# Two-layer decoder trunk: smaller first weight pieces with nine warming products, and an output by block transposes with a feature-major last slice

## Chip, cores and metric

One Trainium2 chip, one core of it. The metric is the device time of one execution in microseconds; of several runs the median counts.

## The reference

The kernel computes a decoder trunk of two layers on 256 tokens of width 2048, in float32. Layer 0 is a gated spatial unit, layer 1 a causal attention of 16 heads (with 256 tokens there is one key block, so the selection of blocks selects nothing). Both end alike, and the change is at the first product of layer 0 and in the end of layer 1:

```
h = x @ w_in                                  # layer 0: parts u, v, z
y = (branch of the layer) * silu(z)
x = layer_norm(ALPHA * x + y @ w_out, g, b)
x = x + sigmoid(x @ w_ple_gate) * (p @ w_ple_proj)
```

## The kernel before, in words

**Products.** Each float32 operand is split into a high part rounded to the float32r type and the low rest. A product is three matrix products into the same PSUM bank: high x high, low x high, high x low (the low x low one is left out). ACT makes the high part with a copy (L121, L75, L314), VectorE the low part by a subtraction (L122, L76, L315).

**Weights.** All weights stream in as 1 MB units in one fixed order (`chunks`, L91 to L106). `load_weights` (L110) brings one unit in pieces, SP issuing the DMAs (L120): four pieces of 512 columns for the first three units, two of 1024 for all others. The raw pieces share four buffers (`wr`, L119), the split forms three (`wh`, `wl`). `weights` (L125) keeps two units ahead of the one in use. The framework orders each engine's instructions by program order and readiness, and puts in the waits.

**Order of work.** `row_unit` (L182) is one weight unit of a product whose result has tokens on the partitions: 24 products of 512 columns. `row_slice` (L222) is four units for one slice of 512 output features (two banks, one for each half of the tokens). `column_unit` (L229) and `feature_product` (L239) are the form whose result has features on the partitions: the weights are the stationary operand, and 512 columns carry the high and the low part of the 256 tokens at once; with `joined` they go one after the other into the same 256 columns. `at(n, f)` runs `f` after n more units (`tick`, L158), which is how transposes, loads and stores are put between products.

**The start.** The identity is made on POOL (L133), then PE runs `WARM` = 7 products on it (L297). `load_x` (L303) loads the first two feature tiles of x one at a time, with the first weight unit between them; the first stage (v of layer 0, L335) runs over the 16 tiles k of the contraction with all eight banks open.

**The end.** In `after` (L450) each layer multiplies by `w_out`, normalises, makes the embedding product (`embed`, L477) and the gate product on the normalised and transposed x (`turn`, L254), then sigmoid, product and sum for each slice (L517 to L529). In layer 0 the result is turned by VectorE in 32x32 blocks and written to DRAM and back by POOL's DMAs (`turn_far`, L265). In layer 1 `store` (L540) turns it back with four PE transposes for 256 features, copies them with ACT and sends two output DMAs from SP (L552); for slices 0 to 2 it runs one and two units later, for the last slice at once. The output is laid out features x tokens.

Of the kernel before, what the change touches and what calls it, by code (L numbers as in the profile page):

```python
# [26 lines left out]
AHEAD = 2  # L27
PARTS = 2
POOL_LO = (0, 1)
WARM = 7  # L30
NT4 = 20
NR4 = 12
NT2 = 5
# [7 lines left out]
def decoder_trunk(ctx: ExitStack, tc: tile.TileContext, xT, pT, wv_a, wu_a, wz_a, w_sT, b_s,  # L41
# [13 lines left out]
    def t2(name):  # L55
        return act.tile([P, 512], F32, name=name, tag="t2", bufs=NT2)
# [8 lines left out]
    def bank(name):  # L65
        return psum.tile([P, 512], F32, name=name, tag="bank", bufs=8)
# [21 lines left out]
    def flat(src):  # L88
        return [("", {}, src.rearrange("p (b e) -> p b e", b=4))]

    chunks = []  # L91
    for k in range(KT):
        chunks += flat(wv_a[k])
# [16 lines left out]
    def load_weights():  # L110
        pat, kw, src = chunks[len(ready)]
        hi = wpool.tile([P, D], F32R, name="wh", tag="wh")
        lo = wpool.tile([P, D], F32R, name="wl", tag="wl")
        parts = 4 if len(ready) < 3 else PARTS
        n = D // parts
        for i in range(parts):
            c = slice(i * n, (i + 1) * n)
            b = slice(i * 4 // parts, (i + 1) * 4 // parts)
            raw = wpool.tile([P, D // PARTS], F32, name="wr", tag="wr", bufs=4)[:, 0:n]  # L119
            nc.sync.dma_start(raw.rearrange("p (b e) -> p b e", b=4 // parts), src[:, b])  # L120
            nc.scalar.activation(hi[:, c], raw, AF.Copy)  # L121
            nc.vector.tensor_sub(lo[:, c], raw, f32(hi[:, c]))  # L122
        ready.append((pat, kw, hi, lo))
# [6 lines left out]
        return w  # L130


    ident = consts.tile([P, P], F32, name="ident")  # L133
    make_identity(nc, ident)
    half = consts.tile([P, NM], F32, name="half")
# [18 lines left out]
    def at(units, f, *args):  # L154

        later.append([units, f, args])
# [25 lines left out]
    def row_unit(banks, ks, xs, order=None):  # L182


        NN = len(banks[0])
        pat, kw, wh, wl = weights()
        if pat:
            wh, wl = ([w.rearrange(pat, **kw)[:, i] for i in range(len(ks))] for w in (wh, wl))
            wh, wl = [[w] for w in wh], [[w] for w in wl]
        else:  # L190
            wh, wl = ([[w.rearrange("p (k n c) -> p k n c", k=len(ks), n=NN)[:, i, n] for n in range(NN)]
                       for i in range(len(ks))] for w in (wh, wl))

        def three(i, m, ns):
            k = ks[i]
            c = slice(m * P, (m + 1) * P)
            xh, xl = xs[k][:, 0, c], xs[k][:, 1, c]
            first, last = k == 0, k == KT - 1

            def o(n):  # L200
                return banks[m][n].rearrange("p (b c) -> p b c", b=4) if pat else banks[m][n]

            for n in ns:
                nc.tensor.matmul(o(n), xh, wh[i][n], start=first, stop=False)  # L204
            for n in ns:
                nc.tensor.matmul(o(n), xl, wh[i][n], start=False, stop=False)  # L206
            for n in ns:
                nc.tensor.matmul(o(n), xh, wl[i][n], start=False, stop=last)  # L208

        if order:  # L210
            for m, n in order:
                for i in range(len(ks)):
                    three(i, m, [n])
        else:
            for i in range(len(ks)):
                for m in range(NM):
                    three(i, m, range(NN))
        tick()
# [3 lines left out]
    def row_slice(xs, name="y"):  # L222

        banks = [[bank(name)] for _ in range(NM)]
        for c in range(4):
            row_unit(banks, range(4 * c, 4 * c + 4), xs, both if c == 3 else None)
        return [b[0] for b in banks]
# [23 lines left out]
        nc.scalar.activation(o, ps[:, 0:S], AF.Copy)  # L251
        nc.vector.tensor_add(o, o, ps[:, S:2 * S])

    def turn(xs, j, rows, n="t"):  # L254

        tp = bank("tp")
        for u in range(2):
            f = 2 * j + u
            for m in range(NM):
                nc.tensor.transpose(tp[:, u * S + m * P:u * S + (m + 1) * P],  # L260
                                    rows[f // 4][:, m, (f % 4) * P:(f % 4 + 1) * P], ident)
        t = split(tp, n)
        xs[2 * j:2 * j + 2] = [t[:, u] for u in range(2)]

    def turn_far(xs, n, rows, name):  # L265

# [29 lines left out]

    warm = bank("warm")  # L297
    for _ in range(WARM):
        nc.tensor.matmul(warm[:, 0:P], ident, ident, start=True, stop=True)

    xs = [None] * KT

    def load_x(k):  # L303
        raw = t2("xr")
        if k:
            nc.sync.dma_start(in2(raw), xT[:, k:k + 2, :])
            t = split(raw, "x")
            xs[k:k + 2] = [t[:, u] for u in range(2)]
            return
        t = t4("x").rearrange("p (k h s) -> p k h s", k=2, h=2)  # L310
        for i in range(2):
            c = raw[:, i * S:(i + 1) * S]
            nc.sync.dma_start(c, xT[:, i, :])
            nc.scalar.activation(t[:, i, 0, :], c, AF.Copy)  # L314
            nc.vector.tensor_sub(t[:, i, 1, :], c, f32(t[:, i, 0, :]))  # L315
            xs[i] = t[:, i]
            if i == 0:
                load_weights()
# [16 lines left out]
    for k in range(KT):  # L335
        order = None
        if k < 2:
            order = [(m, n) for n in range(NS) for m in range(NM)]
        elif k == KT - 1:
            order = [(m, n) for m in range(NM) for n in range(NS)]  # L340
        row_unit(vb, (k,), xs, order)
        if k % 2 == 0 and k + 2 < KT:
            load_x(k + 2)
# [106 lines left out]
    def after(i, br):  # L450
# [26 lines left out]
        def embed(n, m):  # L477
            if m == 0:
                pp.append(r4("pp"))
                if n % 2 == 0:  # L480
                    wp[:] = [t.rearrange("p (k n c) -> p k n c", k=2, n=2) for t in weights(1 + n // 2)[2:]]
            ps = bank("pp")
            c = slice(m * P, (m + 1) * P)
            for k in range(2):
                xh, xl = pk[:, k, 0, c], pk[:, k, 1, c]
                nc.tensor.matmul(ps, xh, wp[0][:, k, n % 2, :], start=k == 0, stop=False)
                nc.tensor.matmul(ps, xl, wp[0][:, k, n % 2, :], start=False, stop=False)
                nc.tensor.matmul(ps, xh, wp[1][:, k, n % 2, :], start=False, stop=k == 1)
            nc.scalar.activation(pp[n][:, m, :], ps, AF.Copy)
# [3 lines left out]
        def norm_slice(n):  # L493
            for m in range(NM):
                normalise(R[n], gb[n], m, mv[:, m, 0:1], rs[:, m:m + 1])

        units = [(n, m) for n in range(NS) for m in range(NM)]
        for u in units[:5]:
            embed(*u)
        for n in range(2):  # L500
            norm_slice(n)
            turn(xn, 2 * n, R, "xn")
            turn(xn, 2 * n + 1, R, "xn")
            if n == 0:
                for u in units[5:]:
                    embed(*u)

        def rest(n):
            norm_slice(n)
            turn(xn, 2 * n, R, "xn")  # L510
            turn(xn, 2 * n + 1, R, "xn")

        at(1, rest, 2)
        at(2, rest, 3)

        xo = [None] * KT
        for n in range(NS):  # L517
            y = row_slice(xn, "g")
            last = i == DEPTH - 1
            for m in range(NM):  # L520
                parts = 2 if last and n == NS - 1 else 1
                w = 512 // parts
                t = t2("sg")
                for h in range(parts):
                    c = slice(h * w, (h + 1) * w)
                    r = R[n][:, m, c]
                    nc.scalar.activation(t[:, c], y[m][:, c], AF.Sigmoid)
                    nc.vector.tensor_mul(t[:, c], t[:, c], pp[n][:, m, c])
                    nc.vector.tensor_add(r, r, t[:, c])  # L529
            if not last:  # L530
                turn_far(xo, n, R, "xt")
                continue
            for h in range(2):
                if n < NS - 1:
                    at(1 + h, store, 2 * n + h)
                else:
                    store(2 * n + h)
        return xo

    def store(j):  # L540

        tp = bank("to")
        for u in range(2):
            f = 2 * j + u
            for m in range(NM):
                nc.tensor.transpose(tp[:, u * S + m * P:u * S + (m + 1) * P],
                                    R[f // 4][:, m, (f % 4) * P:(f % 4 + 1) * P], ident)
        t = t2("o")
        nc.scalar.activation(t, tp, AF.Copy)
        for u in range(2):  # L550
            f = 2 * j + u
            nc.sync.dma_start(out[f * P:(f + 1) * P, :], t[:, u * S:(u + 1) * S])  # L552

    xs = after(0, br)

# [145 lines left out]
```

## Time and profile before

| what | value |
|---|---|
| median of 3 runs | 1047.32 us (1047.27 to 1048.29) |
| profiled execution, its own time | 1048.48 us |
| its span, first to last instruction | 1046.8 us |
| PE busy | 1035.7 us, 99% |
| VectorE (DVE), ScalarE (ACT), GpSimd (POOL) busy | 650.3, 496.0, 70.2 us |
| DMA, mean over the span | 202 GB/s |

How to read it: times are in us from the start of the span. PE is the matrix product, PEld the load of its stationary operand, which runs beside it; SPq is SP's queue, which issues DMAs. A product's row gives start and duration, and products overlap: the distance between starts is what one costs. What ends an engine's idle time stands in brackets as its releaser. Durations are those of one profiled execution.

### The profile page before, as it was taken

Reading aid. Unit: us, or ns where it says so; the run is one execution under the profiler, and the core shown is the slowest. Engines: PE = TensorE matmul, PEld = TensorE weight load, DVE = VectorE, ACT = ScalarE, POOL = GpSimd, SP = SyncE. Lnnn points to the kernel's source line nnn. Section 1 sums busy time; section 2 is a strip of 40 time slices with the busy share of each in tenths; the row PEclk is TensorE's granted clock in tenths of the full one; section 3 lists DMA queues with packets and bytes.
Section 4 is the critical chain, followed back from the end, with each engine's and each line's share of the span. In section 5 each row is a group of like instructions: output and inputs, shape, how many; then the busy total and the mean of one; then the engine's idle time right before and its main releaser. Section 6 shows DMA issues by size and latency. Waiting matters only on the chain.

```text
span 1046.8 us, 13390 instructions
## 1 busy us (share of the span) xinstructions
PE 1035.7 (99%) x5080; PEld 872.0 (83%) x5080; DVE 650.3 (62%) x849; ACT 496.0 (47%) x679; POOL 70.2 (7%) x116
## 2 busy tenths in 40 slices
PE   8999999999999999999999999999999999999997
PEld 6888888888888878888888888888888888888886
DVE  5666774566465696675546666666666555568552
ACT  5545444444353364543435455555555443345442
POOL 1100100023300002233000000000000000000000
PEclk9999999999999999999999999999999999999999
DMA  7775777678965546779655545545555555554651
GB/s 258 261 250 186 254 216 219 190 214 264 298 218 201 195 166 197 252 235 286 232 189 179 180 162 169 171 163 163 172 175 175 199 195 192 188 199 163 208 195 41
DMA packets 104144, 211.23 MB, mean 202 GB/s; under 512 B 25312, under 2 KB 27632, under 8 KB 104080
## 3 DMA queue, kind: packets, MB, share of 16 engines
q1 hardware_dynamic: 99152, 196.64, 57.2%
q0 software_dynamic: 4928, 13.74, 4.7%
q8 instruction: 40, 0.66, 0.3%
q14 instruction: 24, 0.20, 0.1%
HBM read 204.53 MB, written 5.82 MB: 201 GB/s over the span
## 4 chain that ended last, share of the span: by engine, by line
issue 53%; PE 36%; DMA 7%; DVE 2%; POOL 1%; ACT 1%; POOLq 0%; SPq 0%; ACTq 0%; DVEq 0%
PE g L206 4%; PE g L204 4%; PE g L208 4%; PE u L206 3%; PE u L204 3%; PE u L208 3%; PE z L204 2%; PE v L206 2%; PE z L208 2%; PE v L208 2%; PE z L206 2%; PE v L204 2%; DMA xt<-xtb 2%; DMA wr<-in_wv_a 2%; DMA xtr<-xt 2%
## 5 line engine op out<-in xcount | busy, mean ns | idle before, releaser
L122 DVE TENSOR_TENSOR wl<-wr,wh 128x1024 fp32r<-128x1024 f32 (+1 forms) x366 | 432.9, 1205 | 269.9 <-ACT wh L121 265.1
L121 ACT ACTIVATE wh<-wr 128x1024 fp32r<-128x1024 f32 (+1 forms) x366 | 371.9, 1040 | 381.2 <-PE y L206 130.9
L247 PE MATMUL f<-xt,wh 128*128 128x512 f32 x768 | 271.0, 396 | 0.0
L247 PE MATMUL f<-xt,wl 128*128 128x256 f32 x768 | 206.2, 279 | 0.0
L247 PEld LDWEIGHTS f<-xt,wh 128*128 128x128 f32 x768 | 143.2, 188 | 29.9
L247 PEld LDWEIGHTS f<-xt,wl 128*128 128x128 f32 x768 | 144.5, 188 | 2.9
L204 PE MATMUL g<-wh,xn 128*128 128x512 f32 x256 | 101.1, 395 | 0.0
L208 PE MATMUL g<-wl,xn 128*128 128x512 f32 x256 | 99.9, 390 | 0.0
L206 PE MATMUL g<-wh,xn 128*128 128x512 f32 x256 | 99.7, 390 | 0.0
L204 PE MATMUL y<-wh,b 128*128 128x512 f32 x160 | 62.2, 389 | 0.0
L206 PE MATMUL y<-wh,b 128*128 128x512 f32 x160 | 62.2, 389 | 0.0
L208 PE MATMUL y<-wl,b 128*128 128x512 f32 x160 | 62.2, 389 | 0.0
L208 PEld LDWEIGHTS g<-wl,xn 128*128 128x128 f32 x256 | 48.1, 188 | 10.1
L206 PEld LDWEIGHTS g<-wh,xn 128*128 128x128 f32 x256 | 48.1, 188 | 9.5
L204 PEld LDWEIGHTS g<-wh,xn 128*128 128x128 f32 x256 | 48.1, 188 | 9.5
L204 PE MATMUL u<-wh,x 128*128 128x512 f32 x128 | 49.9, 390 | 0.0
L206 PE MATMUL u<-wh,x 128*128 128x512 f32 x128 | 49.9, 390 | 0.0
L204 PE MATMUL z<-wh,x 128*128 128x512 f32 x128 | 49.8, 389 | 0.0
L206 PE MATMUL z<-wh,x 128*128 128x512 f32 x128 | 49.8, 389 | 0.0
L208 PE MATMUL u<-wl,x 128*128 128x512 f32 x128 | 49.8, 389 | 0.0
L208 PE MATMUL z<-wl,x 128*128 128x512 f32 x128 | 49.8, 389 | 0.0
L204 PE MATMUL v<-wh,x 128*128 128x512 f32 x128 | 38.7, 399 | 2.3 <-ACT wh L121 2.3
(156 smaller groups left out, 1398.0 us busy)
## 6 DMA issues: line engine op xcount, KB each, us to landing
wr<-in_wqkz_b SPq DMA_DIRECT2D x96, 512.0 KB, 3.6
wr<-in_w_out SPq DMA_DIRECT2D x64, 512.0 KB, 4.5
wr<-in_w_gate SPq DMA_DIRECT2D x64, 512.0 KB, 4.4
wr<-in_wu_a SPq DMA_DIRECT2D x32, 512.0 KB, 4.5
wr<-in_wz_a SPq DMA_DIRECT2D x32, 512.0 KB, 5.1
wr<-in_wv_b SPq DMA_DIRECT2D x32, 512.0 KB, 4.8
wr<-in_wv_a SPq DMA_DIRECT2D x26, 512.0 KB, 5.1
gb<-vecs POOLq DMA_DIRECT2D x24, 256.0 KB, 8.0
```

The source lines that it names most:

```text
L121: nc.scalar.activation(hi[:, c], raw, AF.Copy)
L122: nc.vector.tensor_sub(lo[:, c], raw, f32(hi[:, c]))
L204: nc.tensor.matmul(o(n), xh, wh[i][n], start=first, stop=False)
L206: nc.tensor.matmul(o(n), xl, wh[i][n], start=False, stop=False)
L208: nc.tensor.matmul(o(n), xh, wl[i][n], start=False, stop=last)
L247: nc.tensor.matmul(*m, start=k == 0 and j == 0, stop=k == KT - 1 and j == len(ms) - 1, skip_group_check=True)
```

## The change

`WARM` goes from 7 to 9, and the warming products run on a tile of ones that VectorE sets, instead of the identity. The first four weight units are loaded into buffers of the larger pool (`r4`, 12 buffers, one piece each); the first in five pieces (256, 256, 512, 512, 512 columns), the next three in two pieces. The first x tile's DMA goes to ACT's queue. The first slice of the first unit is done in two halves of 256 columns. At the end, slices 0 to 2 are turned by VectorE block transposes and stored by POOL DMAs straight to the output. The last slice is computed feature-major: its embedding, its gate product (two banks with high and low columns side by side, two joined), and a kept transposed copy of the normalised x; it is stored by four DMAs from SP. `store` is gone.

```diff
-WARM = 7
+WARM = 9
+    FIRST = (0, 256, 512, 1024, 1536, D)
...
-        parts = 4 if len(ready) < 3 else PARTS
-        n = D // parts
-        for i in range(parts):
-            c = slice(i * n, (i + 1) * n)
-            b = slice(i * 4 // parts, (i + 1) * 4 // parts)
-            raw = wpool.tile([P, D // PARTS], F32, name="wr", tag="wr", bufs=4)[:, 0:n]
-            nc.sync.dma_start(raw.rearrange("p (b e) -> p b e", b=4 // parts), src[:, b])
+        early = len(ready) < 4
+        bounds = FIRST if not ready else range(0, D + 1, D // PARTS)
+        for c0, c1 in zip(bounds, bounds[1:]):
+            c = slice(c0, c1)
+            raw = r4("wr0").rearrange("p m c -> p (m c)") if early else wpool.tile(
+                [P, D // PARTS], F32, name="wr", tag="wr", bufs=4)
+            raw = raw[:, 0:c1 - c0]
+            if early:
+                nc.sync.dma_start(raw, src.rearrange("p b e -> p (b e)")[:, c])
+            else:
+                nc.sync.dma_start(raw.rearrange("p (b e) -> p b e", e=512), src[:, c0 // 512:c1 // 512])
...
+    ones = consts.tile([P, P], F32, name="ones")
+    nc.vector.memset(ones, 1.0)
...
+            if cols:
+                w = [t[i][ns[0]][:, cols] for t in (wh, wl)]
+                for j, (x, y) in enumerate(((xh, w[0]), (xl, w[0]), (xh, w[1]))):
+                    nc.tensor.matmul(o(ns[0])[:, cols], x, y, start=cols.start == 0 and j == 0, stop=False,
+                                     skip_group_check=True)
+                return
...
-    def turn(xs, j, rows, n="t"):
+    def turn(xs, j, rows, n="t", keep=None):
...
+        if keep is not None:
+            nc.scalar.activation(keep[j // 2][:, j % 2, :], tp, AF.Copy)
...
-        nc.tensor.matmul(warm[:, 0:P], ident, ident, start=True, stop=True)
+        nc.tensor.matmul(warm[:, 0:P], ones, ones, start=True, stop=True)
...
-            nc.sync.dma_start(c, xT[:, i, :])
+            (nc.sync if i else nc.scalar).dma_start(c, xT[:, i, :])
...
+            if k == 0:
+                order[0:NM] = [(m, 0, slice(c, c + S)) for c in (0, S) for m in range(NM)]
...
+        def embed_features(n, m):
...
+            ps = bank("pp")
+            for u in range(2):
+                o = ps[:, u * S:(u + 1) * S]
+                c = slice((2 * m + u) * P, (2 * m + u + 1) * P)
+                for k in range(2):
+                    wh, wl = (w[:, k, n % 2, c] for w in wp)
+                    nc.tensor.matmul(o, wh, pk[:, k, 0, :], start=k == 0, stop=False)
+                    nc.tensor.matmul(o, wh, pk[:, k, 1, :], start=False, stop=False)
+                    nc.tensor.matmul(o, wl, pk[:, k, 0, :], start=False, stop=k == 1)
+            nc.scalar.activation(pp[n][:, m, :], ps, AF.Copy)
...
         for n in range(NS):
+            if last and n == NS - 1:
+                final_slice(n, xn, keep[n], pp[n])
+                return
             y = row_slice(xn, "g")
...
+                if last:
+                    store_blocks(n, m, r)
...
+    def store_blocks(n, m, r):
+        t = t2("ob")
+        nc.vector.transpose(t, r)
+        for g in range(4):
+            c = slice(m * P + 32 * g, m * P + 32 * g + 32)
+            nc.gpsimd.dma_start(out[512 * n:512 * n + 512, c].rearrange("(b c) t -> c b t", c=32),
+                              t[32 * g:32 * g + 32, :].rearrange("p (b t) -> p b t", t=32))
+
+    def final_slice(n, xn, r, pp):
+        banks = [bank("g") for _ in range(4)]
+        joined = [b >= 2 for b in range(4)]
+        for c in range(4):
+            pat, kw, wh, wl = weights()
+            wh, wl = (w.rearrange("p (b k c) -> p b k c", **kw) for w in (wh, wl))
+            ks = range(4)
+            if c < 3:
+                for k in ks:
+                    for b in range(4):
+                        feature_product(banks[b], wh[:, b, k, :], wl[:, b, k, :], xn, 4 * c + k, joined[b])
+                tick()
                 continue
+            for b in range(4):
+                for k in ks:
+                    feature_product(banks[b], wh[:, b, k, :], wl[:, b, k, :], xn, 4 * c + k, joined[b])
+            tick()
+        qs = [t2("sg")[:, 0:S] for _ in range(4)]
+
+        def finish(b):
+            q = qs[b]
+            x = r[:, b // 2, (b % 2) * S:(b % 2 + 1) * S]
+            nc.scalar.activation(q, banks[b][:, 0:S] if joined[b] else q, AF.Sigmoid)
+            nc.vector.tensor_mul(q, q, pp[:, b // 2, (b % 2) * S:(b % 2 + 1) * S])
+            nc.vector.tensor_add(x, x, q)
+            f = 4 * n + b
+            nc.sync.dma_start(out[f * P:(f + 1) * P, :], x)
+
+        for b in range(2):
+            halves_sum(qs[b], banks[b])
+        for b in range(4):
+            finish(b)
```

## Rows read from the trace of the kernel before

**Rows 1.** Waits of the whole run: engine, line, waited for, us in total, times, longest.

```profile
PE v L204 <- ACT wh L121: 2.3, 3, 1.1
PE warm L299 <- POOL ident masks.py:199: 1.6, 1, 1.6
PE to L546 <- DVE r L529: 1.4, 1, 1.4
```

**Rows 2.** Timeline, first 14 us: start, duration, engine, line, operation, idle before and releaser.

```profile
0.80 0.20 POOL masks.py:197 MEMSET ident<- 128x128 f32 x1 [0.29 <-POOLq L693]
0.81 1.28 ACT L314 ACT_TABLE_LOAD   x1 [0.81 <-PEq L693]
0.81 0.38 SPq L313 DMA_DIRECT2D xr<-in_xT  x1
...
1.57 3.35 PE L299 MATMUL warm<-ident 128*128 128x128 f32 x14 [1.57 <-POOL ident masks.py:199]
...
3.12 0.42 ACT L314 ACTIVATE x<-xr 128x256 fp32r<-128x256 f32 x1 [1.02 <-DMA xr<-in_xT]
...
5.03 0.63 ACT L121 ACTIVATE wh<-wr 128x512 fp32r<-128x512 f32 x1 [1.50 <-DMA wr<-in_wv_a]
...
5.71 0.80 PE L204 MATMUL v<-wh,x 128*128 128x512 f32 x1 [0.78 <-ACT wh L121]
...
9.72 0.46 PE L204 MATMUL v<-wh,x 128*128 128x512 f32 x1
```

**Rows 3.** Windows, start: length, busy us (count) of PE, PEld, DVE, ACT, POOL, clock, DMA, GB/s.

```profile
2.00:8.00 6.00, 5.22 (x19) 4.41 (x19) 2.49 (x4) 3.01 (x7) 2.13 (x6) 1.00 0.90 302
8.00:10.00 2.00, 2.00 (x6) 1.58 (x5) 1.94 (x5) 1.58 (x4) 0.00 (x0) 1.00 0.89 276
```

**Rows 4.** Timeline of PE, where the second stage (u) begins.

```profile
97.02 0.39 PE L204 MATMUL u<-wh,x 128*128 128x512 f32 x1
...
100.42 0.39 PE L204 MATMUL u<-wh,x 128*128 128x512 f32 x1
```

**Rows 5.** Timeline of PE, last stage: the last product before each of two stores.

```profile
1022.00 0.39 PE L208 MATMUL g<-wl,xn 128*128 128x512 f32 x1
...
1027.92 0.39 PE L208 MATMUL g<-wl,xn 128*128 128x512 f32 x1
```

**Rows 6.** Timeline of PE in the feature-major stage, and its weight loads (ns min/median/max).

```profile
640.58 0.69 PE L618 MATMUL ov<-pb,vk 128*128 128x256 f32 x5
641.11 0.45 PE L247 MATMUL f<-xt,wh 128*128 128x512 f32 x1
641.40 0.28 PE L247 MATMUL f<-xt,wl 128*128 128x256 f32 x1
...
643.14 0.28 PE L247 MATMUL f<-xt,wl 128*128 128x256 f32 x1
```

```profile
L247 PEld LDWEIGHTS f<-xt,wl x768: 187/188/192, 554.9 to 846.5; 128*128 128x128 f32 x192
```

**Rows 7.** The chain that ended last, its end; then the output DMAs of the tile out.

```profile
1039.72 0.39 ACT sg L527
...
1040.13 0.76 DVE sg L528 x2
```

```profile
L552 SPq DMA_DIRECT2D out<-o x16: 332/410/1460, 978.3 to 1043.8; - x16
...
DMA to landing us min/median/max: 1.7/1.8/3.4
```

**Rows 8.** Tile xtb, the block transposes of layer 0; then a window of the last stage.

```profile
L277 POOL DMA_DIRECT2D xt<-xtb x32: 648/651/709, 403.6 to 475.8; - x32
L273 DVE STREAM_TRANSPOSE xtb<-r x8: 711/711/712, 402.6 to 472.9; 128x512 f32<-128x512 f32 x8
...
DMA to landing us min/median/max: 2.3/4.1/6.1
```

```profile
972.00:994.00 22.00, 22.00 (x102) 18.22 (x101) 12.21 (x12) 9.43 (x12) 0.00 (x0) 1.00 0.63 206
```

More of the change, by code (lines that the diff above doesn't have):

```diff
@@ L192, in row_unit, with three @@
                        for i in range(len(ks))] for w in (wh, wl))
-        def three(i, m, ns):
+        def three(i, m, ns, cols=None):
             k = ks[i]
@@ L201, in o @@
                 return banks[m][n].rearrange("p (b c) -> p b c", b=4) if pat else banks[m][n]
+            if cols:
[4 more added lines that the diff above has]
+                return
             for n in ns:
-                nc.tensor.matmul(o(n), xh, wh[i][n], start=first, stop=False)
+                nc.tensor.matmul(o(n), xh, wh[i][n], start=first, stop=False, skip_group_check=NN == NS)
             for n in ns:
-                nc.tensor.matmul(o(n), xl, wh[i][n], start=False, stop=False)
+                nc.tensor.matmul(o(n), xl, wh[i][n], start=False, stop=False, skip_group_check=NN == NS)
             for n in ns:
-                nc.tensor.matmul(o(n), xh, wl[i][n], start=False, stop=last)
+                nc.tensor.matmul(o(n), xh, wl[i][n], start=False, stop=last, skip_group_check=NN == NS)
         if order:
-            for m, n in order:
+            for m, n, *cols in order:
                 for i in range(len(ks)):
-                    three(i, m, [n])
+                    three(i, m, [n], *cols)
         else:
@@ L495, in norm_slice @@
                 normalise(R[n], gb[n], m, mv[:, m, 0:1], rs[:, m:m + 1])
+        def embed_features(n, m):
+            if m == 0:
+                pp.append(r4("pp"))
+                if n % 2 == 0:
+                    wp[:] = [t.rearrange("p (k n c) -> p k n c", k=2, n=2) for t in weights(1 + n // 2)[2:]]
+            ps = bank("pp")
[8 more added lines that the diff above has]
+            nc.scalar.activation(pp[n][:, m, :], ps, AF.Copy)
@@ L497, in after, with fill, turn_slice @@
+        last = i == DEPTH - 1
+        def fill(n, m):
+            (embed_features if last and n == NS - 1 else embed)(n, m)
         units = [(n, m) for n in range(NS) for m in range(NM)]
         for u in units[:5]:
-            embed(*u)
+            fill(*u)
+        keep = [None] * NS
+        def turn_slice(n):
+            norm_slice(n)
+            end = last and n == NS - 1
+            if end:
+                keep[n] = r4("xf")
+            turn(xn, 2 * n, R, "xn", keep if end else None)
+            turn(xn, 2 * n + 1, R, "xn", keep if end else None)
@@ L500, in after @@
         for n in range(2):
-            norm_slice(n)
-            turn(xn, 2 * n, R, "xn")
-            turn(xn, 2 * n + 1, R, "xn")
+            turn_slice(n)
             if n == 0:
                 for u in units[5:]:
[L506 to L514, printed above, removed]
+                    fill(*u)
+        at(1, turn_slice, 2)
+        at(2, turn_slice, 3)
@@ L516, in after @@
         xo = [None] * KT
         for n in range(NS):
+            if last and n == NS - 1:
+                final_slice(n, xn, keep[n], pp[n])
+                return
             y = row_slice(xn, "g")
-            last = i == DEPTH - 1
             for m in range(NM):
-                parts = 2 if last and n == NS - 1 else 1
-                w = 512 // parts
                 t = t2("sg")
[L524 to L529, printed above, removed]
+                r = R[n][:, m, :]
+                nc.scalar.activation(t, y[m], AF.Sigmoid)
+                nc.vector.tensor_mul(t, t, pp[n][:, m, :])
+                nc.vector.tensor_add(r, r, t)
+                if last:
+                    store_blocks(n, m, r)
@@ L530, in after @@
             if not last:
                 turn_far(xo, n, R, "xt")
-                continue
[L533 to L552, printed above, removed]
+        return xo
```

## The prediction, made before the changed kernel ran

> **What bounds the kernel now.** I read the windows first, then the waits of PE, then the timeline at both ends. In a stretch of the last gate stage PE is busy 22.00 of 22.00 us [rows 8], so in the middle of the kernel only PE's own work counts. The waits of PE [rows 1] lie at its two ends: 1.6 us before the warming products, 2.3 us in the first stage in three pieces, 1.4 us before the last transposes; a fourth, in the layer norms, the change leaves alone.
>
> The start [rows 2]: the warming products wait for the identity that POOL makes and begin at 1.57. They are over at 4.92, and the first real product comes at 5.71, when the first 256 KB weight piece has landed and ACT has rounded it (5.03 plus 0.63). From there nine products of 512 columns start before 9.72, one in about 0.43 us, which is 1.2 GHz; later ones start every 0.2267 us (15 between the two rows of [rows 4]), which is 2.4 GHz. The clock column prints 1.00 all along [rows 3], so the level is read from the spacing.
>
> How late is PE by the end of the first stage? It has 16 weight rows x 24 = 384 products, 87.05 us at 0.2267, and the next stage starts at 97.02 [rows 4]: 9.97 us late. Of that 5.71 is the wait for the first product; nine products in 4.01 us instead of 2.04 are 2.0; the two later waits for ACT (2.3 less the 0.8 before 5.71) are 1.5; the rest, 0.7, goes in restarts.
>
> The end [rows 7]: after the last product the chain is sigmoid 0.39, two VectorE products and the sums, six transposes, two copies, four output DMAs one behind the other. From the sigmoid's start at 1039.72 to the end of the span (1046.8) it is 7.1 us; the last output DMA starts at 1043.8, 3.0 us before the end.
>
> **Part 1, the start.** The ones are set by VectorE, which has nothing before them. POOL's memset of the same size starts at 0.80 and takes 0.20 [rows 2], so PE begins near 1.05. Seven products took 3.35 us, 0.48 each; nine take 4.3 and end near 5.35, but as a product starts about 0.2 before its predecessor's end (0.39 long, 0.2267 apart [rows 4]) the first real one can start at **5.1**.
>
> Are its data there? The x piece (128 KB) was issued at 0.81 and used at 3.12. Now it leaves on ACT's queue while a 128 KB weight piece leaves on SP's at the same moment. The second 131 KB at the 302 GB/s of [rows 3] add 0.43: both by 3.55. ACT rounds them in 0.42 each: 4.4. If ACT's table load of 1.28 stands ahead of its DMA, x lands near 4.4 and the piece is ready at 5.25, 0.15 late. The bounds are 5.1 and 5.7, no gain at all; I take 5.1.
>
> The slow level: no row decides when the clock rises once the break between 4.92 and 5.71 is gone. At one end it rises with the first real product and costs 0. At the other it rises at 9.72 as before: 4.6 us of slow products cost 2.2. I take the middle, 1.1. The six first products split into twelve of half the columns cost 0.1 by [rows 6].
>
> The later waits: the first pieces had to share four raw buffers, so SP held them back; now the eleven pieces of the first four rows have buffers of their own (of the larger pool, idle then), and SP issues them without a wait. The bytes up to the first half of row 1 (1.84 MB) flow at 302 GB/s from 2.0 [rows 3] and land near 8.1; ACT needs twice the 0.63 of a piece half as large [rows 2], VectorE about as long, so both forms are ready near 10.7. Row 1 is wanted near 11.6 (5.1, 24 products of 0.2267 and the 1.1). Row 2 and the x that goes with it come with 1 to 2 us to spare. I put 0.3 for waits; the bounds are 0 and the 1.5 of before. Queued behind these pieces on SP is only what is wanted later.
>
> Late after the change: 5.1 + 1.1 + 0.3 + 0.1 = 6.6 instead of 9.97: **gain 3.4**, between 0.2 (5.7, 2.2, 1.5, the restarts) and 4.9.
>
> **Part 2, stores of slices 0 to 2.** Six times four transposes leave PE. Between the two L208 rows of [rows 5] lie 24 products and one store: 5.92 us, where 24 x 0.2267 is 5.44. A store costs 0.48, its restart included; six are **2.9 gained**. At nothing I cost what takes their place. VectorE gets six block transposes of 0.71 (the same operation in layer 0 [rows 8]); weight differences queue behind them, but VectorE is busy 12.21 of 22 us there, and the weights run two units ahead. POOL gets 24 DMA issues of 0.65, 15.6 us, in a stage where it is idle. SP loses twelve stores, and with them its waits for ACT, ahead of weight loads that nobody was late for. ACT loses eight copies and gets two (the kept transposes). Without that cover a late weight row would stop PE; the same layout in layer 0 shows no wait of PE [rows 1, 8].
>
> Those stores write runs of 128 bytes. The row shows 4.1 us for 64 KB in layer 0 [rows 8] against 1.8 for 128 KB in the old stores [rows 7]. The Trainium skill (DMA: Bandwidth & Descriptors, Specifications) says that transfers below 512 bytes cost a read-modify-write; the trace agrees that they are slow, and by that page alone the last gate stage could lose what part 2 gives. The sum goes by the rows: slice 3 takes some 22 us, the last stores before it 4.1 to 6.1 [rows 8], so none of them ends last.
>
> **Part 3, the last slice, feature-major.** Same columns, more and shorter products. For b below 2 there are 32 pairs of 512 and 256 columns; five pairs take 1.74 us [rows 6], 0.348 against 0.340 for 768 columns in the old form: 32 x 0.008 = 0.26. For the joined ones, 96 products of 256: the attention's five (four of 256, one of 128) take 0.53 from start to start [rows 6], 0.118 per 256 columns, so 32 x (0.354 - 0.340) = 0.45. The embedding of that slice: 24 x 0.118 less 12 x 0.2267 = 0.11. Together **0.8 lost**, between 0 and 1.6.
>
> **Part 4, the tail.** After the last product: sigmoid 0.39, product 0.38, sum 0.38, with handoffs 1.2 us; then one DMA, 3.0 from issue to the end as before. The other three blocks are done during the last products (each bank's last ones take 1.4 us). 4.2 instead of 7.1: **2.9 gained**, between 1.3 (a landing of 3.4 instead of 1.8 [rows 7]) and 3.2.
>
> **Sum.** 3.4 + 2.9 - 0.8 + 2.9 = 8.4 us. The profiled execution took 1048.48 us (span 1046.8): 1040.1. The median of the three runs shown is 1.16 lower, 1047.32; I take that difference as common to both kernels and forecast **1038.9**. If it lies in the slow level of the start, up to 1.2 of the gain is missing.
>
> **Rivals.**
> - *The start gives nothing*: the weight stream, not the held-back issue, sets the first stage's waits, and the clock rises no sooner. For it: 302 and 276 GB/s were moved [rows 3] in the very stretch before PE's waits for weights. Against it: PE needs 1 MB of weights in 5.44 us, 193 GB/s. Gain 8.4 - 3.2 = 5.2: 1042.1. Also the case in which the warming does not do what it is for.
> - *Weight loads show* (slower). The last slice has 160 products instead of 96 and its embedding 24 instead of 12: 76 more weight loads of 0.188 us [rows 6]. If they can't hide behind products of 256 columns they cost 14.3 in the place of the 0.8: -5.1, 1052.4. Over the 152 short products the gain is used up from a spacing of 0.118 + 0.055 = 0.17 us on. Against it: the five attention products each load weights of their own and keep 0.118. The Trainium skill (TensorE: Matmul & The Clock Gate, Part 3, What overlaps and what doesn't) states that a load overlaps running products only where the row group differs, and gives 107 ns a load (LDWEIGHTS); an estimate by that page is 8.1 lost, a gain of 1.1. The trace disagrees: 0.188 of load and 0.213 of columns fit in a spacing of 0.2267.
> - *Block stores hold up weights*: short runs on the same DMA engines give back the 2.9 of part 2: 1041.8. Against it: layer 0, above.
>
> **How the numbers follow.** Forecast 0.82, start gives nothing 0.10, block stores 0.03, weight loads 0.03, several small shortfalls together 0.02. A measurement of this kernel tells 0.2% (2.1 us) from no change. So faster 0.95, same 0.02, slower 0.03. The terms' bounds, not all at one end, make 1036.5 to 1041.5 for the forecast; taken up to the first rival with a little beyond, and off the unlikely low end, the range is 1036.8 to 1042.6.
>
> **What would show it.** Warming from near 1.05; the first real product near 5.1 with no break before it; the first row of the next stage near 93.6 instead of 97.02; no wait for ACT between 10 and 30 us; 24 products per weight unit in 5.44 us in slices 1 and 2; the last slice 0.7 longer; 4.2 us from the last sigmoid to the end. A first stage that still ends near 97, or 256-column products over 0.13 apart, would make the prediction wrong.

## The result, and the profile after

| | before | changed |
|---|---|---|
| median (range, runs) | 1047.3 us (1046.51 to 1048.29, 6) | 1041.32 us (1040.80 to 1041.55, 6) |
| profiled execution, own time | 1048.48 us | 1041.33 us |
| its span | 1046.8 us | 1039.6 us |

The ratio is 0.9944 (0.9934 to 0.9954): 6.0 us faster, inside the range, 2.4 us short of the forecast 1038.9. The profiled execution of before stood 1.16 us above its median; that of the changed kernel stands at its own.

The waits of PE, which answer to [rows 1]:

```profile
PE tp L276 <- DVE r L380: 1.1, 2, 0.6
PE warm L317 <- DVE ones L141: 1.1, 1, 1.1
PE v L223 <- DVE wl L129: 0.5, 1, 0.5
PE v L219 <- ACT wh L128: 0.5, 1, 0.5
```

The wait at the end (1.4 us, for the last sums) is gone, the one ahead of the warming products is 0.5 shorter, and the one in the layer norms (tp) is left. The first stage still waits, now twice and half a microsecond each. Where, the timeline of the first 14 us shows, which answers to [rows 2]:

```profile
0.80 0.40 ACTq L331 DMA_DIRECT2D xr<-in_xT  x1
...
1.12 4.21 PE L317 MATMUL warm<-ones 128*128 128x128 f32 x18 [1.12 <-DVE ones L141]
...
1.23 1.28 ACT L332 ACT_TABLE_LOAD   x1 [1.23 <-PEq L760]
...
3.78 0.42 ACT L332 ACTIVATE x<-xr 128x256 fp32r<-128x256 f32 x1 [1.26 <-DMA xr<-in_xT]
...
4.98 1.16 PE L215 MATMUL v<-wh,x 128*128 128x256 f32 x4
...
5.98 0.40 PE L215 MATMUL v<-wl,x 128*128 128x256 f32 x2
...
6.93 0.40 PE L219 MATMUL v<-wh,x 128*128 128x512 f32 x1
...
8.30 0.63 ACT L128 ACTIVATE wh<-wr 128x512 fp32r<-128x512 f32 x1 [2.13 <-DMA wr<-in_wv_a]
...
8.99 0.50 PE L219 MATMUL v<-wh,x 128*128 128x512 f32 x1 [0.50 <-ACT wh L128]
...
11.11 1.06 ACT L128 ACTIVATE wh<-wr 128x1024 fp32r<-128x1024 f32 x1 [0.93 <-DMA wr<-in_wv_a]
...
13.49 0.50 PE L223 MATMUL v<-wl,x 128*128 128x512 f32 x1 [0.53 <-DVE wl L129]
...
13.82 0.39 PE L219 MATMUL v<-wh,x 128*128 128x512 f32 x1
```

The x piece leaves ahead of ACT's table load, the warming begins at 1.12, and the first real product follows it at 4.98 without a break. From about 5.9 the short products come every 0.12 us: the 2.4 GHz level, long before the 9.72 of [rows 2]. Then PE catches up with its weights. ACT sits idle for 2.13 us until the fourth piece lands and rounds it at 8.30; the first half of the next row, which I had landing near 8.1, is rounded only from 11.11. From 6.93 to 13.82 PE takes 6.89 us for 21 steps that cost 4.76 at 0.2267.

The windows of the same stretch, columns as in [rows 3], and the first product of the next stage (97.02 in [rows 4]):

```profile
2.00:8.00 6.00, 6.00 (x33) 5.82 (x33) 1.79 (x4) 2.18 (x5) 1.91 (x6) 1.00 0.84 239
8.00:10.00 2.00, 1.50 (x6) 0.64 (x5) 0.78 (x2) 1.38 (x3) 0.00 (x0) 1.00 1.00 369
```

```profile
94.77 0.39 PE L219 MATMUL u<-wh,x 128*128 128x512 f32 x1
```

In 2:8 the DMA engines moved 239 GB/s, not the 302 of before, and were busy 0.84 of the stretch. The first stage ends 2.25 us earlier than in the profile of before, where I forecast 3.4.

The end, first the chain that ended last (start, duration), then the output's two kinds of stores with their landing, which answer to [rows 7, 8]:

```profile
1027.94 7.61 PE g L262 x54
1035.55 0.02 issue
1035.57 0.39 ACT sg L610
1035.96 0.02 issue
1035.99 0.43 DVE sg L611
1036.42 0.03 issue
1036.45 0.42 DVE xf L612
```

```profile
L584 POOL DMA_DIRECT2D out<-ob x24: 648/650/705, 970.1 to 1020.2; - x24
L614 SPq DMA_DIRECT2D out<-xf x4: 332/358/431, 1033.5 to 1036.9; - x4
```

```profile
L581 DVE STREAM_TRANSPOSE ob<-r x6: 711/711/714, 969.1 to 1017.3; 128x512 f32<-128x512 f32 x6
...
DMA to landing us min/median/max: 2.3/2.8/4.9
```

From the last sigmoid at 1035.57 to the end of the span it is 4.0 us instead of 7.1. The block stores are over long before it: issued by 1020.9, landing 4.9 us at most.

By the profiles, span against span (7.2 us): the start gave 2.25, the tail 3.05, and the middle, from 94.77 to 1035.57 against 97.02 to 1039.72, 1.90.

### The profile page after: what moved, and what is told of

Read it like the earlier page. It is cut to its first block, busy times and chain, and to the rows that moved or that the text cites. A ratio compares the mean times of both kernels' runs of the same rounds, so it can differ in the third digit from the quotient of the medians.

```text
span 1039.6 us, 13497 instructions
## 1 busy us (share of the span) xinstructions
PE 1032.2 (99%) x5134; PEld 873.0 (84%) x5134; DVE 653.2 (63%) x855; ACT 492.2 (47%) x672; POOL 84.0 (8%) x140
## 4 chain that ended last, share of the span: by engine, by line
issue 44%; PE 9%; DMA 3%; DVE 2%; POOL 1%; ACT 0%; POOLq 0%; DVEq 0%
PE g L262 2%; PE g L223 2%; PE g L221 2%; PE g L219 2%; DMA xtr<-xt 2%; DMA xt<-xtb 1%; DVE wl L129 0%; POOL xt L295 0%; PE tp L276 0%; DVE xt L76 0%; DVE sg L569 0%; DVE r L570 0%; DVE xtb L291 0%; ACT xt L75 0%; POOL rs L491 0%
## 5 line engine op out<-in xcount | busy, mean ns | idle before, releaser
L219 PE MATMUL g<-wh,xn 128*128 128x512 f32 x224 | 87.9, 393 | 0.0
L223 PE MATMUL g<-wl,xn 128*128 128x512 f32 x224 | 87.2, 389 | 0.0
L221 PE MATMUL g<-wh,xn 128*128 128x512 f32 x224 | 87.2, 389 | 0.0
L223 PEld LDWEIGHTS g<-wl,xn 128*128 128x128 f32 x224 | 42.0, 188 | 8.8
L221 PEld LDWEIGHTS g<-wh,xn 128*128 128x128 f32 x224 | 42.1, 188 | 8.5
L219 PEld LDWEIGHTS g<-wh,xn 128*128 128x128 f32 x224 | 42.1, 188 | 8.4
L491 POOL TENSOR_TENSOR rs<-rs,half 128x2 f32<-128x2 f32 x2 | 2.3, 1146 | 541.2 <-DVE rs L490 541.2
```

The costliest lines, as they stand in the source:

```text
L223: nc.tensor.matmul(o(n), xh, wl[i][n], start=False, stop=last, skip_group_check=NN == NS)
L491: nc.gpsimd.tensor_tensor(rs, rs, half, op=ALU.pow)
```

## The experiments

Each kernel was timed beside the kernel before; "changed" is the kernel of the change, 1041.32.

**The two halves apart.** The changed start with the old end, and the old start with the changed end:

```diff
-                if last:
-                    store_blocks(n, m, r)
+            for h in range(2):
+                if n < NS - 1:
+                    at(1 + h, store, 2 * n + h)
+                else:
+                    store(2 * n + h)
...
-    def final_slice(n, xn, r, pp):
...
```

> The changed start with the old end. My theory: the change's gain is three separate pieces, in the two profiles 2.25 us at the start (second stage begins at 94.77 instead of 97.02), 1.9 in the middle and 3.05 in the tail. Then the second stage begins near 94.8 here, and the rest of the run is the old one: 1.1 to 2.3 us faster than before (1045.0 to 1046.2), the lower figure if the profile of before drew a slow start. Rival: the start's gain is lost again behind, because PE only waits elsewhere: the same time as before. Rival 2: the start is worth the 3.4 us forecast: 1043.9.

Measured: 1046.49 us (1045.61 to 1047.37, 11 runs), ratio 0.9991 (0.9982 to 1.0). The start alone gains 0.8 us by the medians, less than I expected and hardly clear of the noise (the interval reaches 1.0), though its profile begins u at 94.76, as the changed kernel's does.

```diff
+                if last:
+                    store_blocks(n, m, r)
...
+    def final_slice(n, xn, r, pp):
...
```

> The old start with the changed end (block stores of slices 0 to 2, feature-major last slice). My theory: 1.9 + 3.05 = 4.95 us faster than before, near 1042.3, with the second stage still beginning near 97. Rival: the two parts need each other, and the end alone gives under 3.5 us (over 1043.8).

Measured: 1042.50 us (1042.42 to 1043.08, 5 runs), ratio 0.9955 (0.9943 to 0.9967): 4.8 us, as expected. The surprise is in its start, whose code is the one of before. Its timeline of PE:

```profile
5.34 0.69 PE L204 MATMUL v<-wh,x 128*128 128x512 f32 x1 [0.41 <-ACT wh L121]
5.87 0.40 PE L206 MATMUL v<-wh,x 128*128 128x512 f32 x1
6.10 0.46 PE L208 MATMUL v<-wl,x 128*128 128x512 f32 x1
6.40 0.40 PE L204 MATMUL v<-wh,x 128*128 128x512 f32 x1
6.63 0.39 PE L206 MATMUL v<-wh,x 128*128 128x512 f32 x1
...
95.45 0.39 PE L204 MATMUL u<-wh,x 128*128 128x512 f32 x1
```

The same start runs at 2.4 GHz from 5.87 on (0.23 us between starts), where the profile of before got there at 9.72, and begins u at 95.45 instead of 97.02. So 1.57 us of the old start differ between two executions of the same code (0.37 of it is the first product, at 5.34 instead of 5.71). Against this draw the changed start (94.77) is worth 0.7.

**Two warming products fewer.**

```diff
-WARM = 9
+WARM = 7
```

> The changed kernel with seven warming products instead of nine; they end 0.9 us earlier, near 4.4, and leave a gap of some 0.5 us before the first real product near 4.9. My theory: the unbroken warming is what lets the products space out at the 2.4 GHz level from 5.98 on; with the gap the 1.2 GHz level lasts longer in some runs, up to near 9.7 as in the kernel before, and costs 0 to 1.9 us, so the median is 0.3 to 1.5 us above the changed kernel and the runs scatter more. Rival: the level rises at the same time, and PE then only waits longer for weights: the same time within 0.3 us.

Measured: 1041.38 us (1041.14 to 1041.81), ratio 0.9944 (0.993 to 0.9957): the same as changed. Seven products end as the data arrive, and the first real one starts at 4.59; the pieces behind it come little sooner (the first half of unit 1 is rounded from 10.80 instead of 11.11).

**Stores by PE again, slices 0 to 2; the last slice stays as changed.**

```diff
-                if last:
-                    store_blocks(n, m, r)
+            if last:
+                for h in range(2):
+                    at(1 + h, store, 2 * n + h)
...
```

> The changed kernel with slices 0 to 2 of the output stored as before, by PE transposes, and the last slice feature-major as in the change. My theory: each of the six stores costs PE 0.48 us, so 2.9 us above the changed kernel (near 1044.2). Rival: the block stores' small runs slow the weights or the tail and give part of it back, so that going back costs under 1.5 us.

Measured: 1044.49 us (1044.29 to 1045.6, 8 runs), ratio 0.9973 (0.9962 to 0.9983). The block stores are worth 3.2 us; the forecast had 2.9.

**The last slice as before, block stores kept.**

```diff
-            (embed_features if last and n == NS - 1 else embed)(n, m)
+            embed(n, m)
...
-                final_slice(n, xn, keep[n], pp[n])
...
+            elif n == NS - 1:
+                for h in range(2):
+                    store(2 * n + h)
```

> The changed kernel with the last slice as before: tokens on the partitions, PE transposes and copies in its tail. Slices 0 to 2 keep the block stores. My theory: the tail is 3.05 us longer, the last slice 1.1 and its embedding 0.1 shorter, so 1.85 us above the changed kernel (near 1043.2). Rival: the longer products of the feature-major form eat what the tail gives: the same within 0.5 us.

Measured: 1043.23 us (1043.02 to 1043.37), ratio 0.9959 (0.9946 to 0.9973): 1.9 slower than changed. Its chain at the end:

```profile
1034.52 0.39 ACT sg L569
...
1034.94 0.76 DVE sg L570 x2
1035.70 0.35 DVE r L571
...
1036.09 0.56 PE to L597 x3
```

From the start of u (94.81) to the last sigmoid it is 939.71 us, in the changed kernel 940.80: feature-major costs 1.1. From there to the end it is 7.0 against 4.0: the tail gives 3.0. The difference, 1.9, is what the medians show.

**What holds the weights of the first stage.** Three kernels tried the causes I thought of first. Units 1 to 3 loaded as before, through the four shared buffers:

```diff
-        early = len(ready) < 4
-        bounds = FIRST if not ready else range(0, D + 1, D // PARTS)
+        early = not ready
+        parts = 4 if len(ready) < 3 else PARTS
+        bounds = FIRST if not ready else range(0, D + 1, D // parts)
```

> The changed kernel, but weight units 1 to 3 loaded as before (four pieces of 512 columns for units 1 and 2, four shared raw buffers), so that SP holds them back. Theory A: the eleven pieces issued at once are what makes the last pieces of unit 0 late (its fourth piece is rounded at 8.30 in the changed kernel, at 7.4 in the kernel before); then the fourth piece is there before 7.6, the wait of PE near 9 goes, and the waits of before near 19 and 26 (together 1.5 us) come back: within 1 us of the changed kernel either way. Rival B: the DMA rate from 3.5 to 7 us (about 200 GB/s) does not depend on what is queued behind; the fourth piece still comes near 8.3, and the time is 1 to 2 us above the changed kernel because both kinds of waits are there.

Measured: 1041.96 us (1041.17 to 1042.61), ratio 0.9948 (0.9935 to 0.996). The fourth piece is rounded at 7.38 instead of 8.30, which fits an early queue that delays it; one execution is little to go by, as the changed start gave 8.12 to 8.82 in three other profiles of this section. PE still waits 0.8 us in two places, and the time is within 1 us of changed. Holding SP back had cost next to nothing.

POOL's two small loads (the column vectors and the spatial bias) moved behind ten units:

```diff
+    at(10, load_small)
```

> The changed kernel with POOL's two small loads (gains and biases, 48 and 8 KB, issued at 1.6 and 2.8 us and under way until about 7.5) put off by ten weight units. Theory A: these loads are what holds the DMA engines near 200 GB/s between 3.5 and 7 us; without them the fourth piece of unit 0 is rounded before 7.2 instead of 8.30, unit 1's first half before 10.2 instead of 11.1, the two waits of PE (0.5 each) and the slips around them go, the second stage begins near 92.9 instead of 94.8, and the time is 1 to 2 us below the changed kernel (1039.3 to 1040.3). Rival B: the slow stretch belongs to the weight DMAs themselves; the pieces land at the same times and the time is the same within 0.3 us.

Measured: 1041.59 us (1041.11 to 1041.98), ratio 0.9943 (0.9931 to 0.9956). It told nothing: the framework orders by readiness, and issued them at 1.98 and 3.20 all the same. So they were tied behind the x of rows 4 and 5, by a write that depends on it:

```diff
+            if k == 4:
+                for o in (colp, bsp):
+                    nc.vector.tensor_scalar(o, raw[:, 0:P], 0.0, None, op0=ALU.mult)
+                nc.gpsimd.dma_start(...)
```

> The changed kernel with POOL's two small loads tied behind the arrival of x for k = 4 (after 12 us), by clearing their tiles with a product of that x and zero; merely moving them in the program had left them at 2.0 and 3.2 us. Theory A: these loads hold the DMA engines near 200 GB/s between 3.5 and 7 us; without them unit 0's fourth piece is rounded before 7.5 instead of 8.30, PE's waits near 9 and 13 go, and the time is 1 to 2 us below the changed kernel. Rival B: the slow stretch belongs to the weight DMAs; the fourth piece stays within 0.5 us of 8.3 and the time within 0.4 us.

Measured: 1041.12 us (1040.71 to 1041.52), ratio 0.9941 (0.9929 to 0.9953). Now the first is issued at 22.0, and the windows are those of the changed kernel:

```profile
2.00:8.00 6.00, 6.00 (x32) 5.87 (x32) 1.79 (x4) 2.18 (x5) 0.24 (x1) 1.00 0.78 243
```

243 GB/s where it was 239, and the fourth piece at 8.34. The small loads are not the cause.

**The shape of the pieces.** The first unit in four pieces of 512 columns, with the products unchanged:

```diff
-    FIRST = (0, 256, 512, 1024, 1536, D)
+    FIRST = (0, 512, 1024, 1536, D)
```

> The changed kernel with the first weight unit in four pieces of 512 columns, without the two of 256. My theory: the first real product waits for 256 KB and comes near 5.4 to 5.7 instead of 4.98, but PE is later held by unit 0's fourth piece and unit 1's first half anyway, so the time is within 0.5 us of the changed kernel. Rival: every tenth lost at the first product is lost at the end: 0.4 to 0.7 us slower.

Measured: 1040.10 us (1039.89 to 1040.38), ratio 0.9929 (0.9917 to 0.9942). It is 1.2 faster than changed (the ranges of the two do not overlap), against what every theory of mine said. Its timeline and windows:

```profile
5.13 1.22 PE L215 MATMUL v<-wh,x 128*128 128x256 f32 x4
...
8.09 0.63 ACT L128 ACTIVATE wh<-wr 128x512 fp32r<-128x512 f32 x1 [1.11 <-DMA wr<-in_wv_a]
...
9.99 1.06 ACT L128 ACTIVATE wh<-wr 128x1024 fp32r<-128x1024 f32 x1 [0.92 <-DMA wr<-in_wv_a]
```

```profile
2.00:8.00 6.00, 6.00 (x30) 5.81 (x30) 2.50 (x4) 2.72 (x5) 1.92 (x6) 1.00 0.94 284
8.00:10.00 2.00, 2.00 (x10) 1.63 (x9) 1.03 (x2) 0.99 (x3) 0.00 (x0) 1.00 1.02 413
```

The first product is 0.15 later, but 284 GB/s flow instead of 239, the next unit's half is rounded at 9.99 instead of 11.11, and no wait of PE in the first stage is left in the list: u begins at 93.66, 1.11 before the changed kernel. A 256-column piece is read in runs of 1 KB a row (256 values of 4 bytes), a 512-column one in runs of 2 KB. To tell the length of the runs from the number of DMAs, one short run kept with four DMAs, and long ones with three:

```diff
+    FIRST = (0, 256, 1024, 1536, D)
```

> The changed kernel with unit 0 in four pieces of 256, 768, 512 and 512 columns: one small piece in front, as many DMAs as the run with four pieces of 512 that took 1040.10. Theory A: what the two small pieces cost is one more DMA in SP's row, 0.46 us later for all that follows; with four DMAs the time is that of the four pieces of 512, 1040.1, or a little below as the first product has its data sooner. Rival B: the 1 KB runs of a small piece are what moves badly; with one of them left the time lies half way, 1040.5 to 1041.

Measured: 1040.72 us (1040.18 to 1041.44), ratio 0.9938 (0.9926 to 0.995). With four DMAs and one 1 KB run it stands half way, 267 GB/s in 2:8 and u at 94.03. That speaks for the runs and against the count alone; but a 768-column piece also changes when each bank's data come, so it is half an answer. Nor can it be the slow transfer of the small pieces alone: most of what is missing is missing from 5 to 8 us (232 GB/s in the changed kernel, 301 with four pieces of 512), when both small pieces are there already (rounded from 4.10).

```diff
+    FIRST = (0, 512, 1024, D)
```

> The changed kernel with unit 0 in three pieces of 512, 512 and 1024 columns. Theory A (number of DMAs in SP's row): everything behind comes another 0.45 us sooner, unit 1's first half is rounded near 9.5 instead of 9.99 with four pieces and 11.11 with five, and the time is 0.2 to 0.5 us below 1040.1. Rival: the last half of unit 0 now comes as one piece that PE wants near 8.8, it waits there, and the time is above 1040.1. Rival 2: PE has no wait left to save, the time is 1040.1 within 0.3 us.

Measured: 1043.37 us (1041.61 to 1044.08), ratio 0.9962 (0.9949 to 0.9976). 294 GB/s, but PE waits 1.1 us for the one large piece, and u begins at 94.88, no sooner than in the changed kernel. The time scatters over 2.5 us: two runs, the profiled one among them, list a granted clock of 1.0 (1041.61, 1042.29), the other three 0.997 or 0.998 (1043.37 to 1044.08). So a piece too large gives the gain away; whether it costs more than that, or the lower clock does, is not shown.

Then the other way, four pieces of 512 for the first two units:

```diff
+    FIRST = (0, 512, 1024, 1536, D)
...
-        bounds = FIRST if not ready else range(0, D + 1, D // PARTS)
+        bounds = FIRST if len(ready) < 2 else range(0, D + 1, D // PARTS)
```

> The changed kernel with the first two weight units in four pieces of 512 columns each (units 2 and 3 in two pieces, all in buffers of their own). This asks whether the gain of the four pieces of 512 (1040.10 against 1041.32) holds in a second kernel, and whether more is to be had. My theory: unit 0 arrives as in that run; unit 1's first quarter is rounded before 9.7 instead of its first half at 9.99, and its low part before 10.6 instead of 12.3, so the one slip left, 0.22 us at the third product of unit 1, goes: 1039.8 to 1040.1. Rival: two more DMAs in SP's row, and shorter runs for unit 1, make unit 2 late, and the time is that of the changed kernel, 1041 or more.

Measured: 1039.86 us (1039.46 to 1040.26, 6 runs), ratio 0.9926 (0.9914 to 0.9938): the lowest of all, 1.5 us faster than the change (against one unit so cut, 0.2, the ranges overlap). The next unit's first quarter is rounded at 8.96, and u begins at 92.71, 0.95 before the kernel with one unit so cut; yet its span is only 0.1 shorter (1038.6 against 1038.7). The waits of PE show 0.3 of it:

```profile
PE y L221 <- DVE b L76: 0.3, 1, 0.3
```

The rest is in slips around it. The two kernels stay 0.95 apart up to the first output product of layer 0 (y) and are level from about 293 on. What comes before is a wait of ACT for p, the embedding's operand (first the kernel with two units so cut, then the one with one):

```profile
286.39 0.63 ACT L75 ACTIVATE p<-pr 128x512 fp32r<-128x512 f32 x1 [10.94 <-DMA pr<-in_pT]
```

```profile
285.58 0.63 ACT L75 ACTIVATE p<-pr 128x512 fp32r<-128x512 f32 x1 [9.18 <-DMA pr<-in_pT]
```

p lands 0.8 later though PE is 0.95 ahead, and the operands and weights that ACT rounds after it come that much closer to their use. This is read from the traces; no run moved that load.

**What sets the end of the first stage.** The traces of these kernels answer it together. In us: the first product, the moment from which ACT rounds the first half of unit 1, the first product that needs the low form of that half, and the first product of u:

| kernel | first product | half rounded from | low form used | u begins |
|---|---|---|---|---|
| changed | 4.98 | 11.11 | 13.49 | 94.77 |
| changed start, old end | 4.98 | 11.10 | 13.47 | 94.76 |
| stores by PE again | 4.63 | 11.07 | 13.45 | 94.77 |
| last slice as before | 4.60 | 11.14 | 13.51 | 94.81 |
| seven warming products | 4.59 | 10.80 | 13.17 | 94.46 |
| pieces of 256, 768, 512, 512 | 4.98 | 10.36 | 12.73 | 94.03 |
| four pieces of 512 | 5.13 | 9.99 | 12.36 | 93.66 |

In each of them the low form is used 2.4 us after the rounding begins, and u begins 83.7 us after it. When the first product starts does not show at all: the first four rows run one start code. The third of them, whose first product is 0.35 earlier than in the profile of the change, waits at the same place for the same thing:

```profile
4.63 0.72 PE L215 MATMUL v<-wh,x 128*128 128x256 f32 x4
...
13.45 0.50 PE L223 MATMUL v<-wl,x 128*128 128x512 f32 x1 [0.53 <-DVE wl L129]
```

With two units in four pieces no product of the stage waits any more: u begins 87.53 after the first product at 5.18, and the products alone are 87.05.

## Why the prediction was right, and where it was not

The sign, the range and three of four parts held. The measured gain fell short of the sum of 8.4 by 2.4, in two places of about equal size.

**Part 1, first product: right, but it bought nothing.** 5.1 forecast, 4.98 measured, and x left ahead of the table load, as taken. By the table above, an earlier first product only makes PE wait longer for the weights behind it.

**Part 1, slow level: 1.1 forecast, about 0.5 measured.** I took the middle of 0 and 2.2; up to 5.9 the products cost about 0.5 more than at 2.4 GHz. By the same table this did not enter the time either: the sum added both to the waits, but PE is held until 13.49 with them or without. And the bound "as before" was itself one draw: the same start reached the level at 9.72 in one execution and at 5.87 in another.

**Part 1, "I put 0.3 for waits": the step that failed.** Waits and slips (gaps too short for the list) cost 2.1 (6.89 less 4.76), as much as the 1.5 of waits and the 0.7 of restarts before; the sum kept 0.3 of the one and, without a reason, nothing of the other. The step let the 1.84 MB up to the first half of unit 1 land near 8.1, at the 302 GB/s of [rows 3]. ACT rounds that half only from 11.11. The window up to there:

```profile
2.00:11.11 9.11, 8.61 (x42) 7.35 (x42) 3.51 (x7) 3.75 (x8) 1.91 (x6) 1.00 0.90 287
```

9.11 us at 287 GB/s are 2.6 MB. So the larger error is not the rate but the bytes: nearly 0.8 MB beyond the 1.84 had moved by then, pieces from behind in the row among them, where the forecast said that queued behind is only what is wanted later, and put it at nothing. At 287 GB/s the 1.84 MB alone would have taken until 8.4 (an estimate from that row). The rate is the smaller part: 239 GB/s up to 8 us. With four pieces of 512 it is 284 there, and the same 2.5 MB or so have moved by 9.99 (316 GB/s from 2.0 on).

The rival that the start gives nothing, because the weight stream and not the held-back issue sets these waits, had the reason right: the kernel that holds units 1 to 3 back lost nothing that could be told. I gave it 0.10, with PE's need of 193 GB/s against it; that mean says nothing on when a single piece lands. Of the signs named, u near 93.6 did not come (94.77), though it did not stay near 97 either; and PE still waits between 10 and 30 us, for VectorE's low form (0.53 at 13.49), where the sign had named ACT alone. The lower bound of this part does not follow from its terms: 5.7, 2.2, 1.5 and 0.7 make 10.1, more than the 9.97 of before, so it is a loss of 0.1 and not a gain of 0.2.

**The 1.16 between profile and median: taken as common to both, and it was not.** The caveat under the sum named it: the slow level of the start. The old start with the changed end, profiled at 1042.42 beside its median of 1042.50, begins u 1.57 sooner than the profile of before; no trace of the kernel before at its median is kept. So the start gained 2.25 by the profiles, but 0.8 by the medians of the start alone. By the profiles it misses 1.15 of the 3.4; the draw of the profile takes the other 1.2.

The Trainium skill (TensorE: Matmul & The Clock Gate, Part 1, The HAM clock gate) says that the same kernel shows a different number of slow products from run to run. The traces agree: 5.87 and 9.72 for one start.

**Part 2, stores: right,** 2.9 forecast, 3.2 measured by itself. What took their place is hidden as costed: in the window of the last gate stage PE is still busy all the time, with VectorE at 13.62 us instead of 12.21.

```profile
967.00:989.00 22.00, 22.00 (x98) 18.21 (x97) 13.62 (x16) 9.70 (x11) 5.21 (x8) 1.00 0.70 217
```

The rival that block stores hold up weights falls: 0.70 of the DMA engines are busy, and no product waits. The Trainium skill (DMA: Bandwidth & Descriptors, Specifications) puts a read-modify-write on runs this short. No run here shows what it costs the engines; at 2.8 us for 64 KB (median) it cost the kernel nothing.

**Part 3, feature-major: 0.8 forecast, 1.1 measured.** The mechanism is right, the size a little off: 256-column products start 0.120 apart, not 0.118 (embedding, then the joined products of the last slice, a row now and then holding several):

```profile
941.79 0.28 PE L530 MATMUL pp<-p,wh 128*128 128x256 f32 x1
941.91 0.28 PE L531 MATMUL pp<-p,wl 128*128 128x256 f32 x1
942.03 0.28 PE L529 MATMUL pp<-p,wh 128*128 128x256 f32 x1
...
1033.21 0.40 PE L262 MATMUL g<-xn,wh 128*128 128x256 f32 x2
1033.45 0.28 PE L262 MATMUL g<-xn,wl 128*128 128x256 f32 x1
1033.57 0.40 PE L262 MATMUL g<-xn,wh 128*128 128x256 f32 x2
```

A group of three takes 0.360 us. The rival in which weight loads show would have needed 0.17 a product. The Trainium skill (TensorE: Matmul & The Clock Gate, Part 3, What overlaps and what doesn't) lets a load overlap only where the row group differs; here each 256-column product has its own load of 0.188 and costs 0.120 in all, so the measurement decides against it.

**Part 4, tail: right,** 2.9 forecast, 3.0 measured.

**What stays open.** That the DMA engines move less with the two 1 KB-run pieces ahead is shown as an effect of the pieces' shape, not as a mechanism: run length and number of DMAs are only half told apart. No run put x's first DMA back on SP's queue, so what that move does by itself is not known. That p's load holds back the kernel with the lowest time is read from its trace alone.

## What to carry to other kernels

When a kernel begins on a stream, cut its first pieces for the rate at which the whole stream then arrives, not for the earliest first product: here 0.15 us given up at the first product brought 1.1 at the next stage. A rate read from the trace does not say when one piece lands: what is queued behind it moves at the same time (2.6 MB had moved where 1.84 were asked for first). And before a start of a few microseconds is costed from one profile, see how far that execution stands from the median: the difference may be the very term that the change claims.

## What was not expected of the hardware

- Two 256-column pieces in the place of one of 512 took the rate of the stretch from 2 to 8 us from 284 to 239 GB/s, with the DMA engines busy 0.84 instead of 0.94; three more profiles of the same start show 249, 239 and 236.
- The moment at which TensorE's products come at 2.4 GHz spacing differed by 3.9 us between two executions of the same start (5.87, 9.72), while the granted clock printed 1.00 in both.
- Two warming products more or less, with the first real product at 4.59 or 4.98, made no difference in time (1041.38 and 1041.32): with the pieces of the change, u begins 83.7 us after ACT starts on unit 1's first half, whatever the first product does.
